# A one-layer RWKV and pooling trunk: the output projection's first weight chunks put into the stream's list, its input loaded within its loop through six buffers, and the embedding's fetch moved back

## The chip, the cores and the metric

The kernel runs on one core of one Trainium2 chip. The metric is the device time of one execution in microseconds; lower is better. The time before is 1112.82 us, the median of three runs (1111.49 to 1113.38).

## The reference, cut to what matters

One layer of a decoder trunk on a sequence of 512 positions with a model width of 2048, in float32:

```python
h = rms_norm(x, norm_g[i])
z = jnp.einsum('btd,dn->btn', h, w_in[i])
...
y = wkv7_scan(rh, wh, kh, vh, kk, ah)            # 16 heads x 64, delta-rule state
y = head_group_norm(y, ln_w[i], ln_b[i])
y_rwkv = (y + bonus.reshape(B, T, D_RWKV)).astype(dt) * jax.nn.silu(g_rwkv)
d = causal_multiscale_pool(u).astype(dt)
y_pool = jnp.einsum('btgc,gcd->btgd', d, w_pool[i]).reshape(B, T, D_POOL)
y_pool = y_pool * pool_scale[i] * jax.nn.silu(g_pool)
y_mix = jnp.concatenate([y_rwkv, y_pool], axis=-1)
x = x + jnp.einsum('btc,cd->btd', y_mix, w_out[i])
gate = jax.nn.sigmoid(jnp.einsum('btd,de->bte', x, w_pg[i]) + b_pg[i])
x = x + gate * jnp.einsum('btq,qd->btd', p[i], w_ple[i])
...
return rms_norm(x, final_g)
```

What matters here is the seam in the middle: `y_mix` (2048 channels by 512 positions) is multiplied by `w_out`, and the result feeds a second product with `w_pg`.

## The kernel before, in words

**Precision.** Each float32 operand of a large product is split in two float32r halves: ScalarE casts the high half (`nc.scalar.copy`, tiles named `whi`, `yhi`, `x2hi`), VectorE subtracts it to get the low half (`wlo`, `ylo`, `x2lo`). `mm3` (line 156 issues its matmuls) then does three matmuls: high by high, high by low, low by high. `wsplit` (lines 127 to 134) loads a weight chunk on SyncE's queue (L129) and splits it; it uses three tags of the pool `wp` (`raw`, `whi`, `wlo`) with four buffers each. `split` (lines 136 to 138) does the two halves for anything else.

**First stage.** x is normalised, transposed and split into `hhi` and `hlo`, 16 chunks of 128 channels by 512 positions. A *stream* then computes the columns of z in units of 128 channels: 16 chunks of 3 matmuls each per unit (`zk`, `zr`, `zv`, `zg` for the RWKV part, `zb` for the pooling part), and among them the embedding product (`pple`, `embed_unit`). The weight chunks of the whole stream stand in the list `plan`, and `chunk` takes them from its head: it loads and splits until the wanted chunk is ready, and two more. `plan` ends with the chunks of `b15` and `wp15`, the last pooling unit.

**Second stage, laid into the first.** For each of 8 pairs of heads (j = 0 to 7) the scan runs in chunks of 64 positions. Its small matmuls wait on VectorE, ScalarE and DMAs, so between them `pump(n)` issues n matmuls of the stream; the n are the constants H1 to H5, HE, HT, HX and the triple HC. `scores(j)` issues the products `pbo` and 32 matmuls `pm` that need the tile `bk` from VectorE (L599), and stores masks (`mt`) to DRAM for the triangular inverse (`invert`). It is called once ahead of the loop and then in `between`, after `pump(H3)` and before `pump_to(H2)`; `pump_to` rounds to a boundary that the sum of the pumps decides. Within this stage matmuls keep the order of the program (`pin`).

**The mixed output y.** Each finished piece goes to the DRAM tensor `yd`: a pooling unit through `sgp` (one buffer, L432), a pair of heads through `yo` (L860). 16 pieces of 128 channels by 512 positions, 256 KB each. The pooling units 14 and 15 end the stream, so their pieces are last in the list `order` = 8 to 13, 0 to 7, 14, 15.

**Third stage, the output projection** (`proj` with `w_out`, tiles `acc_o`): four column blocks `ec` of 512 columns. For each, 16 weight chunks in the sequence of `order`; for each chunk 4 row tiles by 3 matmuls, 12 in all. Weight chunks are loaded by `wsplit` in `proj`. The input comes back from `yd` with `load_y`: a DMA into `yin` (three buffers), then the split into `yhi` and `ylo`, which hold all 16 pieces. The first four loads are issued on SyncE's queue ahead of the stream's last pump (`pump(10 ** 6)`), the other twelve on ScalarE's queue behind it. After each block x is added, the sum is stored (`x2d`) and turned (`turn`: transposes `px` and a split into `x2hi`, `x2lo`).

**Fourth stage, the gate** (`proj` with `w_pg`, tiles `acc_g`): again four blocks. The turn of the last output block is laid behind the third chunk of the first gate block (`aside`). `recall` fetches a block of the embedding product back from DRAM (`pler`, four DMAs on ScalarE's queue, L971); block 0 is fetched after the last output block's sums in the program.

**Order.** A scheduler sets the order on each engine from the program's order, its dependences and its buffers; an instruction can so stand well ahead of its place in the text. In the built program the fetch of block 0 stands on ScalarE's queue ahead of the first cast of y. `tc.issue_after` puts what is issued in its block behind a named instruction of the same engine.

Of the kernel before, what the change touches and what calls it, by code (L numbers as in the profile page):

```python
# [9 lines left out]
F32 = mybir.dt.float32  # L10
# [5 lines left out]
P = 128  # L16
T = 512
D = 2048
KT = D // P
# [15 lines left out]
def trunk_kernel(ctx: ExitStack, tc: tile.TileContext, x, p, norm_g, w_in, mu, w0, w_up, a0, a_up,  # L35
                 k_k, k_a, r_k, ln_w, ln_b, w_pool, pool_scale, w_out, w_ple, w_pg, b_pg, final_g, out):
    nc = tc.nc
    PSUM = bass.MemoryType.PSUM
    x, p, w_in, w_out, w_ple, w_pg = x[0], p[0, 0], w_in[0], w_out[0], w_ple[0], w_pg[0]
    out = out[0]  # L40
# [93 lines left out]
        return hi, lo  # L134

    def split(hi, lo, src):
        nc.scalar.copy(hi, src)
        nc.vector.tensor_tensor(lo, src, hi.bitcast(F32), ALU.subtract)


    def rsqrt(y, v, t):
# [27 lines left out]
    plan, ready = [], {}  # L169
# [5 lines left out]
    def chunk(nm, c, ahead=2):  # L175
        while (nm, c) not in ready or ahead > 0:
            if (nm, c) in ready:
                ahead -= 1
            if not plan:
                break  # L180
            n_, c_, src, kt, w_ = plan.pop(0)
            if (n_, c_) not in ready:
                ready[n_, c_] = wsplit(src, kt, w_, f"{n_}_{c_}")
        return ready.pop((nm, c))

    yd = dram.tile([KT, P, T], F32, name="yd", bufs=1)
# [6 lines left out]
    EC = 512  # L193
# [12 lines left out]
    for kind, nm, j in jobs:  # L206
        if kind == "z":
            plan_cols({"r": O_R, "k": O_K, "v": O_V, "g": O_G}[nm] + j * P, f"{nm}{j}")
        elif kind == "p":
            continue  # L210
        elif kind == "e":
            for k in range(2):
                plan.append((f"e{j}_{k}", 0, w_ple[k * P:(k + 1) * P, j * EC:(j + 1) * EC].unsqueeze(1), 1, EC))
        else:
            g, i = j // 4, j % 2
            if j % 4 < 2:
                plan_cols(O_U + g * 256 + i * P, f"b{j}")
            else:
                plan_cols(O_GP + g * 256 + i * P, f"b{j}")
                plan.append((f"wp{j}", 0, w_pool[0, g, :, i * P:(i + 1) * P].rearrange("(k p) n -> p k n", p=P), 2, P))  # L220

    lraw = []

# [42 lines left out]
    pt = psM.tile([P, T], F32, name="pt_prm", tag="m")  # L266
# [38 lines left out]
    pt = psM.tile([P, T], F32, name="pt_prm", tag="m")  # L305
# [202 lines left out]

    pws, kks, late = {}, {}, [None]

    H1, H2, H3, H4, H5, HE = 6, 16, 16, 8, 13, 32

    def decay_and_rate(j):

# [390 lines left out]
    ymp = sy.enter_context(tc.tile_pool(name="ymp", bufs=1))  # L905
    yhi = ymp.tile([P, KT, T], F32R, name="yhi")
    ylo = ymp.tile([P, KT, T], F32R, name="ylo")
    order = [8, 9, 10, 11, 12, 13, 0, 1, 2, 3, 4, 5, 6, 7, 14, 15]

    def load_y(k, queue):  # L910
        t_ = ymp.tile([P, T], F32, name=f"yin{k}", tag="yin", bufs=3)
        queue.dma_start(out=t_, in_=yd[k])
        split(yhi[:, k, :], ylo[:, k, :], t_)

    for k in order[:4]:
        load_y(k, nc.sync)
    pump(10 ** 6)
    pin[0] = False
    for k in order[4:]:
        load_y(k, nc.scalar)  # L920


    x2hi = hp.tile([P, KT, T], F32R, name="x2hi", tag="ahi")
# [2 lines left out]
    KEEP = 8  # L926
# [8 lines left out]
    def proj(w, hi_, lo_, ec, nm, ks=range(KT), tts=range(NT), keep=None, aside=None):  # L935
        acc = {tt: acc_tile(f"acc_{nm}{ec}_{tt}") for tt in tts}
        if keep is not None:
            acc = {tt: [acc[tt]] if tt < NT - 1 else [acc[tt][:, 0:EC // 2], acc_tile("acc_h")[:, 0:EC // 2]]
                   for tt in tts}
        for i, k in enumerate(ks):  # L940
            src = w[k * P:(k + 1) * P, ec * EC:(ec + 1) * EC].unsqueeze(1)
            if keep is None or i < KT - KEEP:
                wh, wl = wsplit(src, 1, EC, f"{nm}{ec}_{k}")
            else:
                raw = wp.tile([P, 1, EC], F32, name=f"raw_{nm}{ec}_{k}", tag="raw")
                nc.sync.dma_start(out=raw, in_=src)
                own = i < KT - 4
                wh = (kp_ if own else wp).tile([P, 1, EC], F32R, name=f"whk{k}", tag=f"whk{k}" if own else "whi")
                wl = (kp_ if own else wp).tile([P, 1, EC], F32R, name=f"wlk{k}", tag=f"wlk{k}" if own else "wlo")
                split(wh, wl, raw)  # L950
                keep[k] = (wh, wl)
                continue
            for tt in tts:
                ts_ = slice(tt * P, (tt + 1) * P)
                parts = acc[tt] if keep is not None else [acc[tt]]
                hw = EC // len(parts)
                for h, a_ in enumerate(parts):
                    hc = slice(h * hw, h * hw + hw)
                    e_ = mm3(a_, hi_[:, k, ts_], lo_[:, k, ts_], wh[:, 0, hc], wl[:, 0, hc], i == 0, i == KT - 1)
            if aside is not None and i == 2:  # L960
                with tc.issue_after(e_.ins):
                    aside()
        return acc

    ples = {}

    def recall(ec, pool):
        ples[ec] = []
        for tt in range(NT):
            t_ = pool.tile([P, EC], F32, name=f"pler{ec}_{tt}", tag="ple", bufs=4)  # L970
            nc.scalar.dma_start(out=t_, in_=pled[tt * P:(tt + 1) * P, ec * EC:(ec + 1) * EC])  # L971
            ples[ec].append(t_)

    for ec in range(D // EC):
        es = slice(ec * EC, (ec + 1) * EC)
        acc = proj(w_out, yhi, ylo, ec, "o", order)
        x2 = []
        for tt in range(NT):
            rows = slice(tt * P, (tt + 1) * P)
            t_ = pp.tile([P, EC], F32, name=f"x2_{ec}_{tt}", tag=("u", "sw")[tt // 2])  # L980
            nc.scalar.dma_start(out=t_, in_=x[rows, es])
            nc.vector.tensor_tensor(t_, acc[tt], t_, ALU.add)
            nc.scalar.dma_start(out=x2d[rows, es], in_=t_)
            x2.append(t_)
        if ec == D // EC - 1:
            recall(0, lp)

        def turn(ec=ec, x2=x2):
            for i in range(EC // P):
                pt = psM.tile([P, T], F32, name=f"px2_{ec}_{i}", tag="m")  # L990
                for tt in range(NT):
                    nc.tensor.transpose(pt[:, tt * P:(tt + 1) * P], x2[tt][:, i * P:(i + 1) * P], ident)  # L992
                split(x2hi[:, 4 * ec + i, :], x2lo[:, 4 * ec + i, :], pt)


        if ec < D // EC - 1:
            turn()
# [4 lines left out]
    with tc.tile_pool(name="fp", bufs=2) as fp, tc.tile_pool(name="kp_", bufs=1) as kp_:  # L1002
# [83 lines left out]
            pre[tt] = (x2_, ple[tt])  # L1086

        for ec in range(LAST):
            ple = ples.pop(ec)
            pre = {}  # L1090
            vec = vectors(ec)
            acc = proj(w_pg, x2hi, x2lo, ec, "g", aside=turn if ec == 0 else None)
            recall(ec + 1, fp if ec % 2 == 0 else lp)
            for tt in range(NT):
                fetch(ec, tt)
                gate(acc[tt], ec, tt, slice(ec * EC, (ec + 1) * EC), ec)
# [60 lines left out]
```

## Time and profile before

| what | value |
|---|---|
| median of three runs | 1112.82 us |
| the profiled execution | 1113.69 us |
| its span, first to last instruction | 1112.0 us |
| TensorE busy | 1076.4 us (97%) |
| VectorE busy | 709.1 us (64%) |
| ScalarE busy | 449.7 us (40%) |
| granted TensorE clock, mean | 0.994 |
| mean DMA rate | 125 GB/s |

One execution is profiled; its own time is the one that terms worked out from its rows belong to. An engine's busy time says little by itself: what counts is where TensorE, the fullest engine, stood still and what it waited for. The views used are the list of waits, the chain of work that ended last (followed back from the last instruction), the timelines of single engines in a window (start, duration, engine, line, operation; in brackets how long the engine was idle before and what ended that), and the table of stretches, whose columns are the length, the busy time and number of instructions of TensorE, its weight loads, VectorE, ScalarE and GpSimd, then the granted clock, the DMAs' share and their rate. A letter q behind an engine's name marks its queue: a wait or the issue of a DMA.

### The profile page before, as it was taken

To read this page: it belongs to the slowest core of one execution; us is meant where nothing else is said; L and a number is where in the kernel's file an instruction comes from. 1 tells how busy PE (TensorE), PEld (TensorE's weight loads), DVE (VectorE), ACT (ScalarE), POOL (GpSimd) and SP (SyncE) were. 2 spreads that over 40 slices of the span, in tenths; PEclk is the share of its full clock that TensorE was granted. 3 is DMA by queue.
4 is the path that set the end of the run, shared out by engine and by line. 5 is a ranking of instruction groups with operands and counts; after the bars stand their busy time and mean duration, and the time that the engine had idled before them with its cause. 6 is when DMAs were issued, how large, how long until landed. Compare 5 with 4: busy or idle time off the path is not lost.

```text
span 1112.0 us, 17260 instructions
## 1 busy us (share of the span) xinstructions
PE 1076.4 (97%) x6090; PEld 879.9 (79%) x6090; DVE 709.1 (64%) x1835; ACT 449.7 (40%) x917; POOL 77.8 (7%) x180
## 2 busy tenths in 40 slices
PE   5999999999999999999999999979999999999996
PEld 4888887887877877877878788768888888888885
DVE  6677868778589688787885957453433324345266
ACT  7633435335335344353352344543222222333246
POOL 2100110110110001201101101000000000000000
PEclk9999999999999999999999999989999999999998
DMA  7433333333423332324234343774434437355444
GB/s 230 119 90 97 102 105 79 103 95 81 119 81 101 103 88 83 98 68 114 76 101 114 88 127 105 241 245 138 162 99 167 155 111 228 111 192 150 135 134 152
DMA packets 178486, 138.56 MB, mean 125 GB/s; under 512 B 34678, under 2 KB 139743, under 8 KB 178399
## 3 DMA queue, kind: packets, MB, share of 16 engines
q1 hardware_dynamic: 158270, 104.94, 32.1%
q10 hardware_dynamic: 20128, 32.52, 9.3%
q8 instruction: 48, 0.79, 0.3%
q14 instruction: 40, 0.32, 0.1%
HBM read 118.02 MB, written 18.87 MB: 123 GB/s over the span
## 4 chain that ended last, share of the span: by engine, by line
PE 48%; ACT 2%; DMA 2%; DVE 1%; issue 0%; ACTq 0%; SPq 0%
PE acc_o L156 16%; PE acc_g L156 14%; PE zb L156 8%; PE pple L156 2%; DMA yin<-yd 1%; PE zr L156 1%; PE zg L156 1%; PE zv L156 1%; PE zk L156 1%; PE py L156 1%; PE px L992 1%; PE pu L156 1%; PE pp L156 1%; ACT L1039 0%; PE ps L156 0%; PE pm L156 0%
## 5 line engine op out<-in xcount | busy, mean ns | idle before, releaser
L133 DVE TENSOR_TENSOR wlo_g<-raw_g,whi_g 128x512 fp32r<-128x512 f32 x88 | 59.6, 685 | 86.2 <-ACT whi_g L132 84.4
L133 DVE TENSOR_TENSOR wlo_o<-raw_o,whi_o 128x512 fp32r<-128x512 f32 x64 | 43.9, 691 | 101.4 <-ACT whi_o L132 101.4
L156 PE MATMUL zb<-hhi,whi_b 128*128 128x512 f32 x256 | 107.0, 418 | 0.0
L156 PE MATMUL acc_o<-whi_o,yhi 128*128 128x512 f32 x256 | 100.2, 395 | 6.8 <-ACT whi_o L132 6.8
L132 ACT CAST whi_g<-raw_g 128x512 fp32r<-128x512 f32 x88 | 54.4, 621 | 115.7 <-PE acc_g L156 71.5
L156 PE MATMUL acc_o<-whi_o,ylo 128*128 128x512 f32 x256 | 100.9, 394 | 0.0
L156 PE MATMUL acc_o<-wlo_o,yhi 128*128 128x512 f32 x256 | 100.5, 393 | 0.0
L156 PE MATMUL zb<-hhi,wlo_b 128*128 128x512 f32 x256 | 100.5, 393 | 0.0
L156 PE MATMUL zb<-hlo,whi_b 128*128 128x512 f32 x256 | 99.9, 390 | 0.0
L156 PE MATMUL acc_g<-whi_g,x2hi 128*128 128x512 f32 (+1 forms) x224 | 86.7, 387 | 0.0
L156 PE MATMUL acc_g<-wlo_g,x2hi 128*128 128x512 f32 (+1 forms) x224 | 86.4, 386 | 0.0
L156 PE MATMUL acc_g<-whi_g,x2lo 128*128 128x512 f32 x224 | 86.0, 386 | 0.0
L132 ACT CAST whi_o<-raw_o 128x512 fp32r<-128x512 f32 x64 | 39.9, 624 | 107.4 <-PE acc_o L156 105.2
L810 POOL TENSOR_SCALAR s0p<-sbd,pw 64x64 f32<-64x64 f32 x96 | 55.9, 582 | 324.0 <-DVE sbd L803 257.7
L132 ACT CAST whi_b<-raw_b 128x512 fp32r<-128x512 f32 x64 | 39.7, 621 | 85.0 <-PE zv L156 34.0
L133 DVE TENSOR_TENSOR wlo_b<-raw_b,whi_b 128x512 fp32r<-128x512 f32 x64 | 43.7, 685 | 33.5 <-ACT whi_b L132 33.2
L156 PEld LDWEIGHTS acc_o<-whi_o,yhi 128*128 128x128 f32 x256 | 48.5, 190 | 16.9 <-ACT whi_o L132 7.2
L156 PEld LDWEIGHTS zb<-hhi,wlo_b 128*128 128x128 f32 x256 | 48.0, 188 | 11.0
L156 PEld LDWEIGHTS acc_o<-wlo_o,yhi 128*128 128x128 f32 x256 | 48.6, 190 | 10.2
L156 PEld LDWEIGHTS acc_o<-whi_o,ylo 128*128 128x128 f32 x256 | 48.6, 190 | 10.0
L655 DVE TENSOR_TENSOR xw<-xw,tm 128x60 f32<-128x60 f32 (+24 forms) x248 | 52.0, 210 | 7.0
L156 PEld LDWEIGHTS zb<-hhi,whi_b 128*128 128x128 f32 x256 | 48.3, 189 | 8.7
(283 smaller groups left out, 2542.7 us busy)
## 6 DMA issues: line engine op xcount, KB each, us to landing
raw_b<-in_w_in_dram SPq DMA_DIRECT2D x64, 256.0 KB
raw_o<-in_w_out_dram SPq DMA_DIRECT2D x64, 256.0 KB
raw_g<-in_w_pg_dram SPq DMA_DIRECT2D x64, 256.0 KB
raw_k<-in_w_in_dram SPq DMA_DIRECT2D x32, 256.0 KB
raw_r<-in_w_in_dram SPq DMA_DIRECT2D x32, 256.0 KB
raw_v<-in_w_in_dram SPq DMA_DIRECT2D x32, 256.0 KB
raw_g<-in_w_in_dram SPq DMA_DIRECT2D x32, 256.0 KB
n<-nd SPq DMA_DIRECT2D x16, 256.0 KB
```

Source lines behind the costliest of these rows:

```text
L132: nc.scalar.copy(hi, raw)
L133: nc.vector.tensor_tensor(lo, raw, hi.bitcast(F32), ALU.subtract)
L156: i = nc.tensor.matmul(*a, **k)
L655: nc.vector.tensor_tensor(xw[:, 0:n_, s + 1:32], xw[:, 0:n_, s + 1:32], tm[:, 0:n_, 0:w_], ALU.add)
L810: nc.gpsimd.tensor_scalar(s0p[hc, :], nxt[hc, hc], pcn[hc], None, ALU.mult)
L992: nc.tensor.transpose(pt[:, tt * P:(tt + 1) * P], x2[tt][:, i * P:(i + 1) * P], ident)
```

## The change

The change has four parts.

1. The first four chunks of `w_out` (8, 9, 10, 11 of block 0) are appended to `plan`, so that `chunk` loads and splits them behind `wp15`; `proj` takes them from there.
2. `load_y` always issues on ScalarE's queue, `yin` has six buffers, and only the first six loads are issued ahead of the stream's last pump. The other ten are issued within the first block's loop, each six chunks ahead of its use.
3. H2 goes from 16 to 12 and H3 from 16 to 20.
4. The fetch of the embedding's block 0 moves from the last output block into the first gate block, behind the last cast of the turn (`split` and `turn` return it).

```diff
     def split(hi, lo, src):
-        nc.scalar.copy(hi, src)
+        c_ = nc.scalar.copy(hi, src)
         nc.vector.tensor_tensor(lo, src, hi.bitcast(F32), ALU.subtract)
+        return c_
...
+    order = [8, 9, 10, 11, 12, 13, 0, 1, 2, 3, 4, 5, 6, 7, 14, 15]
+    for k in order[:4]:
+        plan.append((f"o0_{k}", 0, w_out[k * P:(k + 1) * P, 0:EC].unsqueeze(1), 1, EC))
...
-    H1, H2, H3, H4, H5, HE = 6, 16, 16, 8, 13, 32
+    H1, H2, H3, H4, H5, HE = 6, 12, 20, 8, 13, 32
...
-    order = [8, 9, 10, 11, 12, 13, 0, 1, 2, 3, 4, 5, 6, 7, 14, 15]
-
-    def load_y(k, queue):
-        t_ = ymp.tile([P, T], F32, name=f"yin{k}", tag="yin", bufs=3)
-        queue.dma_start(out=t_, in_=yd[k])
+    AHEAD = 6
+
+    def load_y(k):
+        t_ = ymp.tile([P, T], F32, name=f"yin{k}", tag="yin", bufs=AHEAD)
+        nc.scalar.dma_start(out=t_, in_=yd[k])
         split(yhi[:, k, :], ylo[:, k, :], t_)
 
-    for k in order[:4]:
-        load_y(k, nc.sync)
+    for k in order[:AHEAD]:
+        load_y(k)
     pump(10 ** 6)
     pin[0] = False
-    for k in order[4:]:
-        load_y(k, nc.scalar)
...
-            if keep is None or i < KT - KEEP:
+            if nm == "o" and ec == 0 and i + AHEAD < KT:
+                load_y(ks[i + AHEAD])
+            if (f"{nm}{ec}_{k}", 0) in ready:
+                wh, wl = ready.pop((f"{nm}{ec}_{k}", 0))
+            elif nm == "o" and ec == 0 and i < 4:
+                wh, wl = chunk(f"{nm}{ec}_{k}", 0)
+            elif keep is None or i < KT - KEEP:
                 wh, wl = wsplit(src, 1, EC, f"{nm}{ec}_{k}")
...
             if aside is not None and i == 2:
                 with tc.issue_after(e_.ins):
-                    aside()
+                    hi = aside()
+                with tc.issue_after(hi.ins):
+                    recall(0, lp)
...
-        if ec == D // EC - 1:
-            recall(0, lp)
-
         def turn(ec=ec, x2=x2):
...
-                split(x2hi[:, 4 * ec + i, :], x2lo[:, 4 * ec + i, :], pt)
+                hi = split(x2hi[:, 4 * ec + i, :], x2lo[:, 4 * ec + i, :], pt)
+            return hi
```

What this does to the order on the engines is shown at three places. The names carry the piece or chunk: `yin12` is the load of piece 12 of y, `whi_o0_9` the high half of chunk 9 for block 0 of the output projection (in the new kernel a chunk of the list has one more number behind it).

ScalarE at the seam, before. The cast of the first chunk, `whi_o0_8`, stands seventeen rows ahead of the cast of the second; these are the last twelve, down to `whi_o0_9`:

```order
L912 DMA yin0_8106<-yd_136 128x512
L912 DMA yin1_8110<-yd_136 128x512
L367 ACTIVATE sgp15_8086<-zb15_8037 128x512
L912 DMA yin2_8114<-yd_136 128x512
L137 CAST yhi_7989<-yin0_8106 128x512
L137 CAST yhi_7989<-yin1_8110 128x512
L432 DMA yd_136<-sgp15_8086 128x512
L137 CAST yhi_7989<-yin2_8114 128x512
L912 DMA yin3_8118<-yd_136 128x512
L912 DMA yin4_8122<-yd_136 128x512
L912 DMA yin5_8126<-yd_136 128x512
L132 CAST whi_o0_9_8173<-raw_o0_9_8171 128x512
```

ScalarE at the same place, now, from the first chunk's cast to the fourth's:

```order
L132 CAST whi_o0_8_0_4871<-raw_o0_8_0_4869 128x512
L918 DMA yin12_8031<-yd_136 128x512
L137 CAST yhi_8013<-yin11_8027 128x512
L918 DMA yin13_8035<-yd_136 128x512
L132 CAST whi_o0_9_0_4921<-raw_o0_9_0_4919 128x512
L137 CAST yhi_8013<-yin12_8031 128x512
L438 DMA yd_136<-sgp14_8057 128x512
L137 CAST yhi_8013<-yin13_8035 128x512
L918 DMA yin0_8137<-yd_136 128x512
L132 CAST whi_o0_10_0_4927<-raw_o0_10_0_4925 128x512
L373 ACTIVATE sgp15_8118<-zb15_8069 128x512
L132 CAST whi_o0_11_0_4955<-raw_o0_11_0_4953 128x512
```

The casts of the four chunks now stand among the casts of the first six pieces of y, and the loads that follow are issued one by one between them. The store of `sgp14` has come behind the cast of piece 12; before it stood ahead of the casts of y.

ScalarE a little later, before, from the fourth chunk's cast to the sixth's:

```order
L132 CAST whi_o0_11_8209<-raw_o0_11_8207 128x512
L137 CAST yhi_7989<-yin6_8130 128x512
L137 CAST yhi_7989<-yin7_8134 128x512
L132 CAST whi_o0_12_8227<-raw_o0_12_8225 128x512
L137 CAST yhi_7989<-yin14_8138 128x512
L912 DMA yin15_8142<-yd_136 128x512
L132 CAST whi_o0_13_8245<-raw_o0_13_8243 128x512
```

ScalarE there now, from the cast of piece 0 to the sixth chunk's cast:

```order
L137 CAST yhi_8013<-yin0_8137 128x512
L918 DMA yin2_8169<-yd_136 128x512
L438 DMA yd_136<-sgp15_8118 128x512
L137 CAST yhi_8013<-yin1_8153 128x512
L918 DMA yin3_8185<-yd_136 128x512
L137 CAST yhi_8013<-yin2_8169 128x512
L918 DMA yin4_8201<-yd_136 128x512
L132 CAST whi_o0_12_8207<-raw_o0_12_8205 128x512
L137 CAST yhi_8013<-yin3_8185 128x512
L918 DMA yin5_8223<-yd_136 128x512
L137 CAST yhi_8013<-yin4_8201 128x512
L132 CAST whi_o0_13_8229<-raw_o0_13_8227 128x512
```

All loads of y but one stood ahead of the fifth chunk's cast (`whi_o0_12`) before; now the loads of pieces 3 and 4 stand just ahead of it, and the loads from piece 5 on behind it.

TensorE behind the seventh call of `scores` (j = 6), before; `pm6` are the last of its matmuls, `zk7` is the stream, whose weight chunk `whi_k7_0` ends here and `whi_k7_1` begins:

```order
L156 MATMUL pm6_10_6130<-ar6_6065,bk6_6066 128x128
L156 MATMUL pm6_11_6131<-ar6_6065,bk6_6066 128x128
L156 MATMUL zk7_6112<-hhi_134,whi_k7_0_3386 128x512
L156 MATMUL zk7_6112<-hlo_135,whi_k7_0_3386 128x512
L156 MATMUL zk7_6112<-hhi_134,wlo_k7_0_3387 128x512
L156 MATMUL zk7_6112<-hhi_134,whi_k7_1_3428 128x512
```

TensorE behind the same call, now:

```order
L157 MATMUL pm6_10_6157<-ar6_6089,bk6_6090 128x128
L157 MATMUL pm6_11_6158<-ar6_6089,bk6_6090 128x128
L157 MATMUL zk7_6136<-hhi_134,whi_k7_1_3428 128x512
L157 MATMUL zk7_6136<-hlo_135,whi_k7_1_3428 128x512
L157 MATMUL zk7_6136<-hhi_134,wlo_k7_1_3429 128x512
```

The last step of `whi_k7_0`, three matmuls, has moved from behind `scores` to ahead of it. One step of the stream moves so at all eight calls; the scan's next product behind it, `py`, stands where it stood.

More of the change, by code (lines that the diff above doesn't have):

```diff
@@ L1088, in trunk_kernel @@
         for ec in range(LAST):
-            ple = ples.pop(ec)
             pre = {}
@@ L1092, in trunk_kernel @@
             acc = proj(w_pg, x2hi, x2lo, ec, "g", aside=turn if ec == 0 else None)
+            ple = ples.pop(ec)
             recall(ec + 1, fp if ec % 2 == 0 else lp)
```

## The prediction

> **What bounds the kernel now.** I read the page first, then the chain that ended last, the waits of TensorE, and the timelines of TensorE, ScalarE and SyncE around the one long wait.
>
> ```profile
> span 1112.0 us, 17260 instructions
> PE 1076.4 (97%) x6090; PEld 879.9 (79%) x6090; DVE 709.1 (64%) x1835; ACT 449.7 (40%) x917; POOL 77.8 (7%) x180
> ```
>
> TensorE (PE) is busy 97% of the span, so all that an edit of order can give lies in the other 3%, 35.6 us, and in stretches where the clock is not full. The profiled execution took 1113.69 us, 1.7 more than its span and 0.9 more than the median of the runs, 1112.82. I make the sum against the profiled time and carry the difference over to the median.
>
> TensorE's waits, longest first (total, times, longest):
>
> ```profile
> PE pt_prm L267 <- DMA ngr<-in_norm_g_dram: 7.0, 1, 7.0
> PE acc_o L156 <- ACT whi_o L132: 6.8, 1, 6.8
> PE pt_h L279 <- DVE xt L263: 3.1, 2, 1.6
> PE pm L156 <- DVE bk L599: 2.3, 3, 1.5
> PE pu L156 <- DVE zs L781: 1.1, 4, 0.4
> ```
>
> The first and the third are the kernel's start, which the change leaves alone. The second is the start of the output projection, where it works; the fourth is `scores`, which H2 and H3 move; the fifth is the scan just behind it. So the change can take away 9.1 us of waiting, and what hangs on it.
>
> The chain over the seam of the two stages (start, duration, what):
>
> ```profile
> 720.89 3.66 DMA yd<-yo
> 725.07 0.42 SPq L912
> 725.54 6.92 DMA yin<-yd
> ...
> 738.91 3.59 DMA yin<-yd
> ...
> 744.27 0.63 ACT whi_o L132
> 744.94 43.26 PE acc_o L156 x180
> ...
> 792.58 41.07 PE acc_o L156 x181
> ```
>
> The chain runs from loads of y through their casts on ScalarE into the cast of a weight chunk. The timeline of TensorE shows which:
>
> ```profile
> 735.28 0.39 PE L156 MATMUL acc_o<-whi_o,yhi 128*128 128x512 f32 x1
> ...
> 744.94 2.08 PE L156 MATMUL acc_o<-whi_o,yhi 128*128 128x512 f32 x4 [6.78 <-ACT whi_o L132]
> ...
> 749.96 0.39 PE L156 MATMUL acc_o<-whi_o,yhi 128*128 128x512 f32 x1
> ```
>
> The projection starts at 735.28 without a wait, does its first chunk, stands still for 6.78, does the second, and begins the third at 749.96. The stretches 738 to 745, 745 to 750 and 750 to 755 (last columns: clock, DMA share, GB/s) say what follows the wait:
>
> ```profile
> 738.00:745.00 7.00, 0.22 (x2) 0.06 (x1) 4.23 (x7) 3.23 (x6) 0.00 (x0) 0.84 0.61 215
> 745.00:750.00 5.00, 5.00 (x13) 3.95 (x14) 3.50 (x6) 2.99 (x5) 0.00 (x0) 0.54 0.75 211
> 750.00:755.00 5.00, 5.00 (x24) 4.14 (x23) 4.23 (x7) 3.39 (x6) 0.00 (x0) 1.00 0.77 265
> ```
>
> After the wait the granted clock is 0.54 for 5 us. A full-speed pitch is 41.07 / 181 = 0.227 us, so two chunks of 12 matmuls cost 5.45. They took 749.96 - 735.28 = 14.68. **The seam costs 9.23 us**: 6.8 of waiting and 2.4 of slow clock.
>
> **The output projection's chunks.** The wait is one of order. In the old order seventeen rows of ScalarE stand between the casts of the first chunk and the second: eight loads of y (which wait for one of three buffers), six casts of y (which wait for landings), a fetch, a store and `sgp15`. In the new order it is three, and the third and fourth chunk follow after four rows and one. The six first loads go out on ScalarE's queue from 724.71, where the embedding's fetch went, under the same wait (for the store of `yo`, which lands at 720.89 + 3.66 = 724.55). SyncE's row, then ScalarE's:
>
> ```profile
> 724.69 1.28 SPq L912 DMA_DIRECT2D yin<-yd  x3
> ...
> 724.71 0.83 ACTq L971 DMA_DIRECT2D pler<-pled  x2
> ...
> 726.13 0.37 ACTq L971 DMA_DIRECT2D pler<-pled  x1
> 730.07 0.62 ACT L137 CAST yhi<-yin 128x512 fp32r<-128x512 f32 x1 [3.54 <-DMA yin<-yd]
> 731.15 0.62 ACT L137 CAST yhi<-yin 128x512 fp32r<-128x512 f32 x1 [0.46 <-DMA yin<-yd]
> 732.48 0.62 ACT L137 CAST yhi<-yin 128x512 fp32r<-128x512 f32 x1 [0.72 <-DMA yin<-yd]
> 733.01 0.62 ACT L132 CAST whi_o<-raw_o 128x512 fp32r<-128x512 f32 x1
> ```
>
> Three loads as late as now would put the first chunk's cast at 733.01 as now, and TensorE starts at 735.28 again. The second chunk's cast needs one more load, sent when the first has landed (row order: cast of yin8, load of yin11). What one trip from issue to cast takes, three at a time:
>
> ```profile
> 732.63 0.33 ACTq L912 DMA_DIRECT2D yin<-yd  x1
> 733.86 0.33 ACTq L912 DMA_DIRECT2D yin<-yd  x1
> 736.53 0.62 ACT L137 CAST yhi<-yin 128x512 fp32r<-128x512 f32 x1 [0.56 <-DMA yin<-yd]
> 737.54 0.62 ACT L137 CAST yhi<-yin 128x512 fp32r<-128x512 f32 x1 [0.38 <-DMA yin<-yd]
> 742.58 1.66 ACTq L912 DMA_DIRECT2D yin<-yd  x3
> 745.33 1.28 ACT L137 CAST yhi<-yin 128x512 fp32r<-128x512 f32 x2 [0.44 <-DMA yin<-yd]
> ```
>
> 3.9, 3.7 and, with less in flight, 2.75; the chain has 3.59. The first load of the burst at 724.7 took 5.4, the third 6.92. So chunk 9 is cast at 724.71 + 5.4 + 3.7 + 0.1 + 0.55 (a cast's pitch) = 734.5 and split by VectorE 1.3 later, 735.8; TensorE wants it at 735.28 + 2.72 = 738.0. Chunk 10, one trip further, is cast by about 739.3 and chunk 11 by 741.6; they are wanted at 740.7 and 743.45. The store of `sgp14` now goes out behind the cast of yin12, at about 736.8, and `sgp15`, in the same buffer, waits the 3.66 that a store takes, with chunk 11 behind it; that is in the 741.6.
>
> **The new wait.** Each later load is issued from the same in-order queue, behind a cast that waits for an earlier load. Chunk 12 hangs on five trips one after another (yin8, 11, 13, 0, 2): 724.71 + 5.4 + 4 x 3.7 + 4 x 0.1 = 745.3, then two casts, 746.5, and VectorE's half, 747.2 (727.0 + 5 L, if every trip takes L). TensorE would want that half at 735.28 + 4 x 2.72 + 0.23 = 746.4: **0.8 lost**. Chunk 13 needs one more trip (yin4, issued with the cast at 745.3), 3.7 for a chunk of 2.72: **1.0 lost** (L - 2.72). From there two loads are in flight at a time, one per 1.9 us, faster than a chunk's 2.72, so it ends. Three of the embedding's four fetches, each as large as a load of y, leave the burst, so its first trip should come nearer to 4.4, which takes the loss to 0.8. Bounds: none at all at 2.75 a trip; about 4.5 if the first takes 6.92 and the others 3.9. I take 1.5, between 0.8 and 1.8, nearer to the rows as they stand. A wait of this size does not slow the clock: after TensorE's wait of 1.51 before `pm` the next matmuls run at 3.62 / 15 = 0.24 us.
>
> ```profile
> 512.04 2.06 PE pm L156 x32
> 514.09 3.62 PE zk L156 x15
> ```
>
> The Trainium skill ("DMA: Bandwidth & Descriptors", section "Issuing engines are not separate DMA queues") says that all issuers share the same 16 DMA engines, and that another issuer only saves the sequencer's issue time. That speaks against this part: the loads' move to ScalarE buys no bandwidth and puts four more issues on the engine that casts. By it the trips stay as the rows have them and the sum stands; if a queue of their own made them 2.75, the 1.5 would go and the sum would be 1102.1. No row here compares the two queues alone.
>
> SyncE loses its four y loads and sends chunks 10 and 11 earlier, which costs nothing. GpSimd has no part in it.
>
> **H2 and H3.** Of 32 matmuls around `scores`, one step of three moves ahead of it, 0.68 us, at eight places. Where `pm` waits for `bk`, the step fills the wait:
>
> ```profile
> 436.34 1.83 PE L156 MATMUL pm<-ar,bk 64*128 64x128 f32 x28 [0.62 <-DVE bk L599]
> 512.04 2.06 PE L156 MATMUL pm<-ar,bk 64*128 64x128 f32 x32 [1.51 <-DVE bk L599]
> ```
>
> The third of the three is 0.2. Gain 0.62 + 0.68 + 0.2 = **1.5 us**. Behind `scores` the masks on VectorE end 0.7 later while `py` stays where it was; the scan's `zs` comes behind them, and TensorE waits for it 1.1 in all today. I take nothing for that. Bounds: from a loss of 1.1, those waits doubled and nothing gained, to the 1.5.
>
> **The embedding's fetch.** Four issues of about 0.4 move on ScalarE to behind the last turn, ahead of the cast of the gate's chunk 7:
>
> ```profile
> 935.24 0.59 ACT L137 CAST x2hi<-px 128x512 fp32r<-128x512 f32 x1
> 937.36 0.62 ACT L132 CAST whi_g<-raw_g 128x512 fp32r<-128x512 f32 x1 [1.53 <-PE acc_g L156]
> 969.20 1.23 ACT L1034 ACTIVATE gt<-gt 128x512 f32<-128x512 f32 x2 [1.36 <-DVE gt L1033]
> ```
>
> That cast waits for the slot of chunk 3; chunks 4 to 6 give TensorE 8 us in which 1.7 are hidden. The fetched tiles are used at 969, over 25 us after. Nothing.
>
> **Sum.** 9.23 (seam) + 1.5 (`scores`) - 1.5 (new waits) = 9.2 us less: 1113.69 becomes 1104.5, and the median 1112.82 becomes **1103.6**.
>
> **Rivals.** (1) *Trips of about 4.5 us.* Then chunk 12 waits 727.0 + 5 x 4.5 - 746.4 = 3.1, chunk 13 another 1.8, and the first wait may be long enough to slow the clock again (2.4). Loss 7.3: 1112.82 - 9.23 - 1.5 + 7.3 = 1109.4. For it: the burst had 5.4 to 6.9, so a trip grows with what is in flight. Against: the y loads quoted after the burst took 3.9 at most. The trace leaves open where between 1.51 and 6.78 the clock gives way. The Trainium skill ("TensorE: Matmul & The Clock Gate", section "What's actually happening") puts it at an idle window of about 3.4 us; by that rule the clock would stay and this case would end at 1107.0.
>
> (2) *The load chain becomes the bound; slower.* Its place is ScalarE's queue from yin11 to yin15. With each trip at L, chunks 12 and 13 lose 6 L - 22.1, and the clock 2.4; that equals the 10.7 gained at L = 5.07. At 6.1, which the burst's second load took (from 725.07 to the cast at 731.15), the loss is 16.9: 1119.0. From 5.4 on, two loads in flight no longer keep up with 2.72 a chunk. Against it: the same rows as in (1), and three fetches fewer in the burst.
>
> (3) *No change.* Trips of just about 5 us give the gain back, or the first chunk itself comes late because it now stands behind casts of y whose loads ScalarE issues. That would need the first cast some 9 us later than 733.01, with fewer transfers ahead of it than now. 1112.8.
>
> **Chances.** Forecast 0.76, with its own range 1101.5 to 1108.1; (1) 0.13; (2) 0.05; (3) 0.06. The bottom is the gain without a new wait, 1102.1, less some of the spread of the runs (1111.49 to 1113.38). The top is 4.5 of waiting and nothing from H3: 1112.82 - 4.7 = 1108.1. That leaves out half of (1), (2) and (3), under 2 in 10. About 0.2%, 2.2 us, is what a measurement of this kernel can tell from no change; faster by more 0.89, within it 0.06, slower 0.05.
>
> **What would show it.** In the new profile: TensorE's wait for `whi_o` of 6.8 gone and no stretch at 0.54 near 745; in its place waits under 1.5 for `whi_o` or `wlo_o` at the fifth and sixth chunk; `pm` waiting 0.8 in all for `bk`; trips of 3 to 4 us from an issue of `yin` to its cast. It is wrong if a single wait of over 3 us stands in the first projection, if the trips take over 4.5, or if TensorE waits anew behind `scores`.

## The result and the profile after

| kernel | median | range | profiled span | mean clock |
|---|---|---|---|---|
| before, beside these runs | 1113.1 us | 1111.49 to 1115.0 | 1112.0 us | 0.994 |
| changed | 1103.03 us | 1102.61 to 1103.82 | 1101.5 us | 0.997 |

The ratio is 0.9904, with a 95% interval from 0.9892 to 0.9917: the change takes 9.2 to 12.0 us away. The changed kernel's profiled execution took 1103.22 us.

Its page, and TensorE's waits in it (total, times, longest):

```profile
span 1101.5 us, 17252 instructions
PE 1074.0 (98%) x6090; PEld 878.4 (80%) x6090; DVE 708.1 (64%) x1835; ACT 448.8 (41%) x917; POOL 77.7 (7%) x180
```

```profile
PE pt_prm L273 <- DMA ngr<-in_norm_g_dram: 6.7, 1, 6.7
PE pt_h L285 <- DVE xt L269: 3.2, 2, 1.6
PE pu L157 <- DVE zs L787: 1.1, 4, 0.4
...
PE pm L157 <- DVE bk L605: 0.8, 1, 0.8
```

The wait of `acc_o` for `whi_o` is gone from the list, and no other wait of `acc_o` is in it. `pm` waits once, 0.8, where it waited three times, 2.3. The scan's 1.1 is as it was, and the two waits of the kernel's start nearly so (6.7 and 3.2; before 7.0 and 3.1). The chain now crosses the seam on TensorE alone, and the stretches around it have the full clock (columns as before; clock, DMA share and GB/s last):

```profile
732.40 1.36 PE pp L157 x6
733.76 43.52 PE acc_o L157 x192
```

```profile
737.00:744.00 7.00, 7.00 (x32) 5.82 (x31) 4.48 (x7) 3.43 (x7) 0.00 (x0) 1.00 0.89 272
744.00:749.00 5.00, 5.00 (x23) 4.13 (x22) 3.78 (x7) 3.56 (x7) 0.00 (x0) 1.00 0.68 209
749.00:754.00 5.00, 5.00 (x24) 4.13 (x23) 2.75 (x6) 2.19 (x4) 0.00 (x0) 1.00 0.74 237
```

43.52 / 192 = 0.227 us, the full-speed pitch from the first chunk on. Where TensorE was busy 0.22 of 7.00 us before, it is busy 7.00 of 7.00.

The matmuls of one kind show the length of the whole projection, by the starts of the first and the last; before, then changed:

```profile
L156 PE MATMUL acc_o<-whi_o,ylo x256: 388/389/628, 735.7 to 924.1; 128*128 128x512 f32 x128
```

```profile
L157 PE MATMUL acc_o<-whi_o,ylo x256: 389/389/481, 734.0 to 913.2; 128*128 128x512 f32 x128
```

By TensorE's timelines, from the start of the first matmul of `acc_o` to that of the last, it is 188.87 us before and 179.63 changed. So the span's 10.46 us split like this: 9.24 inside the projection, 1.68 ahead of it (first matmul at 735.28, now 733.60; the stream's first matmuls start within 0.02 us of each other), and 0.46 lost behind it (from the last matmul to the end 187.82, now 188.28).

### The profile page after: what moved, and what is told of

It reads as the page before. It is cut to its first block, busy times and chain, and to the rows that moved or that the text cites. A ratio compares the mean times of both kernels' runs of the same rounds, so it can differ in the third digit from the quotient of the medians.

```text
span 1101.5 us, 17252 instructions
## 1 busy us (share of the span) xinstructions
PE 1074.0 (98%) x6090; PEld 878.4 (80%) x6090; DVE 708.1 (64%) x1835; ACT 448.8 (41%) x917; POOL 77.7 (7%) x180
## 4 chain that ended last, share of the span: by engine, by line
PE 67%; DVE 4%; ACT 3%; DMA 1%; issue 1%; ACTq 0%; DVEq 0%
PE acc_o L157 16%; PE acc_g L157 13%; PE zb L157 13%; PE zg L157 5%; PE zk L157 4%; PE zr L157 4%; PE zv L157 2%; PE py L157 2%; PE pu L157 1%; PE pp L157 1%; PE pm L157 1%; PE pple L157 1%; DMA pled<-ple 1%; PE ps L157 1%; DVE xw L661 1%
```

## The experiments

Each is read by its median and by the length of the projection as just defined, which is that of its one profiled execution. The ratio is to runs of the kernel before that were taken beside the experiment; their median was 1113.82 us for e1 to e4, 1114.05 for e5 to e8 and 1113.71 for e9 to e12, and 1113.1 beside the changed kernel. So a difference between medians of two such groups can be off by up to about 0.9 us.

| run | what it is | median, us | ratio to before, 95% interval | projection, us |
|---|---|---|---|---|
| changed | all four parts | 1103.03 | 0.9892 to 0.9917 | 179.63 |
| e1 | list alone | 1109.5 | 0.9945 to 0.997 | 184.51 |
| e2 | loop and six buffers alone | 1106.18 | 0.9916 to 0.9941 | 180.30 |
| e3 | changed, H2 and H3 as before | 1104.34 | 0.9898 to 0.9925 | 179.63 |
| e4 | H2 and H3 alone | 1112.8 | 0.9976 to 0.9994 | 189.83 |
| e5 | list, fetch | 1106.99 | 0.9921 to 0.9948 | 182.38 |
| e6 | list, six buffers | 1114.82 | 0.9999 to 1.0017 | 189.24 |
| e7 | changed, more DMA traffic | 1115.39 | 0.9997 to 1.0015 | 188.52 |
| e8 | changed, H2, H3 = 8, 24 | 1104.37 | 0.9903 to 0.993 | 180.15 |
| e9 | changed, fetch in its old place | 1103.55 | 0.9892 to 0.9919 | 180.15 |
| e10 | changed, three buffers | 1102.63 | 0.9889 to 0.9916 | 179.63 |
| e11 | list, six buffers, fetch | 1111.08 | 0.9958 to 0.9982 | 186.32 |
| e12 | changed, H2, H3 = 10, 22 | 1102.7 | 0.9887 to 0.9914 | 179.75 |

The theory is the prediction's: what counts is the order of ScalarE, that is, how many casts of y, each hanging on a landing, stand ahead of the cast of the weight chunk that TensorE wants next. The rivals are the transfers themselves (their length in the burst) and the number of buffers.

### e1: the list alone

```diff
+    for k in order[:4]:
+        plan.append((f"o0_{k}", 0, w_out[k * P:(k + 1) * P, 0:EC].unsqueeze(1), 1, EC))
...
+            if (f"{nm}{ec}_{k}", 0) in ready:
+                wh, wl = ready.pop((f"{nm}{ec}_{k}", 0))
+            elif nm == "o" and ec == 0 and i < 4:
+                wh, wl = chunk(f"{nm}{ec}_{k}", 0)
```

> The kernel before with the first part of the change alone: the four weight chunks end the stream's list; y is loaded as before (three buffers, four loads on SyncE), H2 and H3 and the fetch are as before. Theory (order): the 6.8 us wait was the second chunk's cast standing behind y loads and y casts that were not needed yet; in this kernel's order the casts of chunks 8 to 11 stand right behind the casts of pieces 10, 10, 13 and 13, so the wait goes, with at most 2 us left around chunks 12 and 13; about 9 us faster than before, 1104 (the 1.5 us of H2 and H3 are not in it). Rival (transfers): the relief came from the loads of y being sent one by one through six buffers and from the fetch having left the burst, so that trips became short; then with three buffers and the fetch in the burst the trips stay at 3.6 to 6.9 us and a wait of 4 us or more remains in the seam; at most 5 us faster, 1108 or more.

It brought 4.36 of the 9.24 us (188.87 to 184.51); 4.88 stayed. TensorE's timeline has two waits for a chunk's cast, at the sixth and at the eighth chunk; the chain shows what the first hangs on:

```profile
750.65 0.51 PE L156 MATMUL acc_o<-whi_o,yhi 128*128 128x512 f32 x1 [1.66 <-ACT whi_o L132]
...
757.94 0.50 PE L156 MATMUL acc_o<-whi_o,yhi 128*128 128x512 f32 x1 [0.82 <-ACT whi_o L132]
```

```profile
725.81 8.00 DMA yin<-yd
733.84 0.63 ACT yhi L137
...
742.92 5.29 DMA yin<-yd
748.24 0.63 ACT yhi L137
```

The list holds four chunks; behind it the casts of y decide again, and the third load of the burst took 8.00 us from issue to landing. So "order alone" was too simple: with long trips the wait comes back four chunks later, though in a smaller size. The time, 1109.5, is the one that the rival named (1108 or more), but without its wait of 4 us or more. The idle times, with those for `wlo_o`, sum to 3.2, but 4.88 were lost. A matmul takes 0.39 and the next starts 0.227 behind it, so a wait, which is counted from the end of the last matmul, costs 0.16 more than it shows; five waits make 0.8. The rest is lost in the matmuls just behind each wait, of which the first takes 0.5 and a later one starts about 0.1 late.

### e2: the loop and six buffers alone

```diff
-        t_ = ymp.tile([P, T], F32, name=f"yin{k}", tag="yin", bufs=3)
-        queue.dma_start(out=t_, in_=yd[k])
+        t_ = ymp.tile([P, T], F32, name=f"yin{k}", tag="yin", bufs=AHEAD)
+        nc.scalar.dma_start(out=t_, in_=yd[k])
...
+            if nm == "o" and ec == 0 and i + AHEAD < KT:
+                load_y(ks[i + AHEAD])
```

> The kernel before with the second part alone: y loaded in the loop through six buffers on ScalarE, no chunks in the list, H2, H3 and fetch as before. Theory (order): in this kernel's order the first chunk's cast stands behind the cast of piece 13, three trips down the chain (4.8 + 2.7 + 2.9 us from 724.7, then the cast and VectorE's half), so TensorE waits 1 to 2.5 us ahead of the first chunk and up to 1 us at the next two; 6 to 8 us faster than before, 1105 to 1107. Rival (transfers): all of the relief comes from this part; no wait over 0.5 us, 9 us faster, 1104.

The first chunk's cast stands behind six casts of y, and TensorE waits for it (the view says only "issue", but that cast runs from 735.54 to 736.16):

```profile
736.26 0.47 PE L156 MATMUL acc_o<-whi_o,yhi 128*128 128x512 f32 x1 [0.99 <-issue]
737.02 0.50 PE L156 MATMUL acc_o<-wlo_o,yhi 128*128 128x512 f32 x1 [0.29 <-DVE wlo_o L133]
```

Behind that there is no wait, as the order theory had it, and 1106.18 lies in its range. So the loop alone takes most of the seam, and the list is worth what is left: 1106.18 - 1104.34 (e3, which adds list and fetch) = 1.8 us.

### e3 and e4: H2 and H3

```diff
-    H1, H2, H3, H4, H5, HE = 6, 12, 20, 8, 13, 32
+    H1, H2, H3, H4, H5, HE = 6, 16, 16, 8, 13, 32
```

> The changed kernel with H2 and H3 back at 16 and 16. Theory: TensorE's wait of pm for bk is 2.3 us again in three places instead of 0.8 in one, everything else as in the changed kernel: 1.5 us slower than the changed kernel, about 1104.5. Rival: what H2 and H3 take from pm they give back elsewhere (masks later on VectorE, so zs or the casts later): 0.5 us or less between the two.

```diff
-    H1, H2, H3, H4, H5, HE = 6, 16, 16, 8, 13, 32
+    H1, H2, H3, H4, H5, HE = 6, 12, 20, 8, 13, 32
```

> The kernel before with H2 = 12 and H3 = 20 alone. Theory: 1.5 us faster than before, pm's wait 0.8 us in one place, the seam's wait of 6.8 us untouched. Rival: 0.5 us or less.

Given the rest, the two numbers are worth 1104.34 - 1103.03 = 1.3 us by the medians, whose ranges lie apart. They are of two such groups, and by the ratios it is 0.9 with overlapping intervals; in the traces both projections are 179.63 long, and the changed kernel's starts 1.51 earlier (735.11 to 733.60), though its stream starts 0.2 later. Alone the two numbers are worth 0.7 to 2.7 us by the ratio. In e4's trace the projection starts 1.9 earlier than before (733.38; 0.3 of it is there at the start of the stream), and its long wait then is 7.05 instead of 6.78 long: a part of what is gained ahead of an unmended wait is lost in it.

### e5: list and fetch

e1, with the fetch behind the turn, as in the change's fourth part.

> The kernel before with the list's four chunks and the embedding's fetch moved back, but three buffers, the loads of y in front of the loop and H2, H3 = 16, 16. The list alone took 1109.5 us: 4.9 us of the seam's 9.2 were still there, in waits of TensorE at the second, sixth and ninth chunk, and the first three trips of y took 6.0, 7.5 and 8.0 us beside four fetches of the embedding. Theory 'burst': the fetches in the burst make those trips long and put the three-buffer chain late; without them the first trips are 4.5 to 5.5 us, the waits go, and the time is 1104 to 1106 us (the changed kernel with H2, H3 = 16, 16 took 1104.34). Rival 'three buffers': each load must wait for a cast to free its buffer, so the chain stays late whatever lies beside it; waits of 2 us or more stay and the time is 1108 to 1110 us.

1106.99 lies between the two theories, and each holds in part. The burst's first trips fell to 4.3, 4.9 and 5.1 us, and 2.1 of e1's 4.88 went. The rest is one wait at the eighth chunk:

```profile
750.13 0.33 ACTq L915 DMA_DIRECT2D yin<-yd  x1
...
755.32 0.62 ACT L137 CAST yhi<-yin 128x512 fp32r<-128x512 f32 x1 [2.77 <-DMA yin<-yd]
...
755.99 0.62 ACT L137 CAST yhi<-yin 128x512 fp32r<-128x512 f32 x1
756.51 1.14 ACT L132 CAST whi_o<-raw_o 128x512 fp32r<-128x512 f32 x2
```

Here fifteen of the sixteen casts of y stand ahead of the eighth chunk's cast, for which TensorE waits 1.0. (The expectation above has e1's waits at the second, sixth and ninth chunk; they are at the third, sixth and eighth.)

### e6 and e11: six buffers without the loop

```diff
-        t_ = ymp.tile([P, T], F32, name=f"yin{k}", tag="yin", bufs=3)
+        t_ = ymp.tile([P, T], F32, name=f"yin{k}", tag="yin", bufs=6)
```

> The kernel before with the list's four chunks and six buffers for y, with the loads still in front of the loop, the fetch at its old place and H2, H3 = 16, 16. ScalarE's order then has the cast of the fifth chunk (12) behind the casts of fifteen of the sixteen tiles of y. Theory 'burst and order': the first trips stay at 6 to 8 us, and the fifth chunk waits for fifteen trips; from the third landing about 9.5 us after the first issue and then one tile in about 1.25 us, the fifth chunk's halves are ready some 25 us after the first issue, about 4 us after TensorE wants them: 1108 to 1112 us, with the wait at the fifth chunk. Rival 'three buffers': the buffers were what held the list back, and the time is 1104 to 1106 us with no wait over 0.5 us.

> The kernel before with the list, six buffers and the fetch moved back, H2, H3 = 16, 16 and the loads of y in front of the loop: all of the change but the loop. ScalarE's order has the cast of the fifth chunk (12) behind fourteen tiles of y. Theory 'order': with list and six buffers alone the fourteenth tile landed 27.4 us after the first was issued, and TensorE waited 7.1 us at the fifth chunk; first trips that are 2 us shorter bring that to some 4 to 5 us: 1108 to 1112 us, slower than with three buffers (1107.0). Rival 'fetch and buffers': both together free the loads, and the time is 1104 to 1106 us.

More buffers made it slower, by 5.3 us against e1 and by 4.1 against e5. ScalarE in e6, ahead of the wait at the fifth chunk, then TensorE there:

```profile
750.50 0.62 ACT L137 CAST yhi<-yin 128x512 fp32r<-128x512 f32 x1 [1.32 <-DMA yin<-yd]
...
752.04 1.27 ACT L137 CAST yhi<-yin 128x512 fp32r<-128x512 f32 x2 [0.92 <-DMA yin<-yd]
753.22 1.13 ACT L132 CAST whi_o<-raw_o 128x512 fp32r<-128x512 f32 x2
```

```profile
753.88 2.07 PE L156 MATMUL acc_o<-whi_o,yhi 128*128 128x512 f32 x4 [7.08 <-ACT whi_o L132]
```

In e11 it is the same place with a shorter wait:

```profile
750.21 2.08 PE L157 MATMUL acc_o<-whi_o,yhi 128*128 128x512 f32 x4 [4.10 <-ACT whi_o L132]
```

With the loads in front of the loop, buffers that are free let the scheduler put fifteen casts of y (e6) or fourteen (e11) ahead of the fifth chunk's cast, where three buffers had let it put eight (e1) or nine (e5). This is the wait of before, moved on by three chunks. So the row at which the cast stands decides where TensorE waits. How long it waits hangs on the trips as well: e1, with eight casts ahead, is slower than e5 with nine. e11 came out as its theory had it. e6's theory had the place, but a wait of about 4 us; it was 7.08, with a granted clock of 0.52 from 754 to 758 behind it, and the time missed the 1108 to 1112.

### e7: more traffic

```diff
+        d_ = ymp.tile([P, 1024], F32, name=f"fl{k}", tag="fl", bufs=2)
+        nc.gpsimd.dma_start(out=d_, in_=w_pg[k * P:(k + 1) * P, 0:1024])
         nc.scalar.dma_start(out=t_, in_=yd[k])
```

> The changed kernel with one more load of 512 KB on GpSimd's queue for each of the sixteen loads of y, into a tile that nothing reads; ScalarE's order is as in the changed kernel. It prices the second rival: what longer trips do. Measured trips of the five that the fifth chunk hangs on were 4.7, 2.6, 2.9, 3.9 and 2.9 us, with nothing waiting. Theory: the margin at the fifth chunk was about 3 us, so trips longer by 1 us each (L from 3.1 to over 4) already eat it, and beyond that each 1 us of trip costs about 5 us at the fifth chunk; trips of 4.5 to 6 us are expected, and 1106 to 1120 us, with waits of TensorE at the fifth and later chunks. Rival: the sixteen engines serve the y loads ahead, trips stay under 4 us, and the time is within 1.5 us of 1103.

The order is the changed kernel's, only the DMA engines are full (share 1.01, 368 GB/s, against 0.85 and 268 in the same stretch of the changed kernel):

```profile
734.00:744.00 10.00, 9.68 (x41) 7.23 (x40) 4.89 (x9) 3.41 (x6) 2.11 (x4) 1.00 1.01 368
...
754.00:758.00 4.00, 3.56 (x8) 2.55 (x9) 2.47 (x4) 1.62 (x4) 1.00 (x2) 0.57 0.98 340
```

```profile
747.66 0.50 PE L157 MATMUL acc_o<-whi_o,yhi 128*128 128x512 f32 x1 [1.65 <-ACT whi_o L132]
748.47 0.50 PE L157 MATMUL acc_o<-wlo_o,yhi 128*128 128x512 f32 x1 [0.31 <-DVE wlo_o L133]
754.43 0.80 PE L157 MATMUL acc_o<-whi_o,yhi 128*128 128x512 f32 x1 [3.17 <-ACT whi_o L132]
```

The five trips that the fifth chunk hangs on took 4.44, 5.32, 4.84, 4.52 and 4.14 us from issue to landing, 4.65 in the mean, and TensorE waits at the fifth and sixth chunk (and 0.3 at the fourth). The projection is 8.9 us longer than in the changed kernel, which eats the seam's gain: the second rival's mechanism, at its place. The weight chunks' loads are slower here too, but the casts that are waited for follow directly behind casts of y.

### e8 and e12: on from H2, H3 = 12, 20

> The changed kernel with H2, H3 = 8, 24 in place of 12, 20. From 16, 16 to 12, 20 the waits of pm for bk fell from 2.3 to 0.8 us and the time fell by 1.3 us. Theory: four more vectors' matmuls ahead of that wait take away the last 0.8 us (at 511 us) too, 0.7 to 1.1 us faster than the changed kernel: 1102.0 to 1102.4. Rival: 8 matmuls are too few behind which the casts and zs can hide, so a wait of pu or pp takes its place: 1103.0 us or more.

> The changed kernel with H2, H3 = 10, 22, between 12, 20 (1103.03 us, pm waits 0.8 us for bk) and 8, 24 (1104.37 us, no wait of pm, but py waits 0.73, 0.48, 0.48 and 0.48 us for mt). Two matmul columns are about 0.45 us of TensorE: pm's wait should fall to about 0.4 us and py's waits to about 0.3 us in all. Theory: the two nearly cancel, 1102.6 to 1103.4 us, not to be told from the changed kernel. Rival: both waits vanish, 1102.2 us or less, a better kernel.

e8's largest new wait, then what is left of `pm`'s in e12:

```profile
PE py L157 <- DVE mt L630: 2.2, 4, 0.7
```

```profile
PE pm L157 <- DVE bk L605: 0.2, 1, 0.2
```

At 8, 24 `pm` no longer waits, but `py` waits for the masks, which come later: 1.3 us slower than 12, 20 by the medians, with ranges that lie apart (1104.16 to 1105.77), though the ratios' intervals overlap. So the theory failed, and the rival's time came, with `py` in the place of `pu` or `pp`. At 10, 22 `py` does not wait for them and `pm` waits 0.2. Its median is 0.3 below the changed kernel's, with overlapping ranges (1102.56 to 1103.04 against 1102.61 to 1103.82), so it can't be called better.

### e9 and e10: the fetch in its old place; three buffers

```diff
-                    hi = aside()
-                with tc.issue_after(hi.ins):
-                    recall(0, lp)
+                    aside()
...
+        if ec == D // EC - 1:
+            recall(0, lp)
```

> The changed kernel with the embedding's fetch back at its old place in the code. Without the loop the fetch sat in the burst of the first loads, and moving it took 2.1 us of the list's waits away (1109.5 to 1107.0 us). With the loop, ScalarE's order has the four fetches behind the last load of y, between the casts of the last chunks. Theory (the prediction's 'embedding's fetch move: nothing'): with the loop in, the place of the fetch in the code changes nothing that TensorE waits for: 1102.5 to 1103.6 us, first trips of y as in the changed kernel (4.7, 5.0, 5.2 us). Rival: the fetch move carries a part of the gain here too, first trips of 6 us or more and 1104.5 to 1106 us.

```diff
-    AHEAD = 6
+    AHEAD = 3
```

> The changed kernel with three buffers for y in place of six, loads still in the loop, three chunks ahead. Theory 'order': what counts is that the cast of each chunk stands behind no more tiles of y than TensorE needs soon; the fifth chunk's cast is behind eight tiles here (ten in the changed kernel), with 8 us of matmuls between a load and its use, so three buffers are enough: 1102.6 to 1104.0 us, no wait of the output projection over 0.5 us. Rival 'buffers': the three buffers that left waits of 1.0 us and more in the kernel with list and fetch alone leave them here too: 1105 to 1107 us.

Neither can be told from the changed kernel (the fifth chunk's cast is behind nine tiles there, not ten as e10's expectation counts). In e9 the fetch stays out of the burst without being moved; ScalarE's timeline:

```profile
723.38 1.30 ACTq L918 DMA_DIRECT2D yin<-yd  x3
...
727.87 0.62 ACT L137 CAST yhi<-yin 128x512 fp32r<-128x512 f32 x1 [2.74 <-DMA yin<-yd]
...
754.17 0.33 ACTq L981 DMA_DIRECT2D pler<-pled  x1
```

Once y's loads stand in the loop on ScalarE's queue, the scheduler puts the fetch behind the last of them, 30 us later. So the fetch is worth 2.5 us (e1 to e5) or 3.7 (e6 to e11) where the loads stand in front of the loop, and nothing measurable where they stand in it. The same holds for the buffers: six cost 4 to 5 us without the loop, and with it three do as well.

## Why the prediction was right, point by point

The predicted 1103.6 is 0.6 above the measured median. The mechanism was right; one term was mis-sized. That the totals lie so near is in part luck. The sum rests on the profiled executions, and there 1104.5 stands beside 1103.22, some 1.3 off: the mis-sized term makes 1.5, but 0.46 was lost behind the projection, for which the sum has nothing. And the profiled execution of before lies 0.9 above its median, that of the changed kernel only 0.2.

**The seam, 9.23.** Measured 9.24 (188.87 to 179.63). That wait and slow clock had to be counted together is shown by the full clock in all three stretches above.

**H2 and H3, 1.5.** 1.3 between the medians of e3 and the changed kernel (0.9 by the ratios), and 1.68 by the projection's start against before. The two waits of 0.62 and 0.2 are gone and 1.51 became 0.82. Nothing was taken for what lies behind `scores`, and the scan's waits are 1.1 as before. e8 shows that this holds for one step: the next one turns into waits of `py`.

**The new waits, -1.5: the step that was mis-sized.** They are 0 in the changed kernel's trace. The step took 5.4 for the first trip and 3.7 for the others. ScalarE in the changed kernel, the five trips to chunk 12 (yin8, 11, 13, 0, 2):

```profile
723.02 1.31 ACTq L918 DMA_DIRECT2D yin<-yd  x3
...
727.77 0.62 ACT L137 CAST yhi<-yin 128x512 fp32r<-128x512 f32 x1 [3.00 <-DMA yin<-yd]
727.78 0.33 ACTq L918 DMA_DIRECT2D yin<-yd  x1
...
730.41 0.63 ACT L137 CAST yhi<-yin 128x512 fp32r<-128x512 f32 x1 [0.17 <-DMA yin<-yd]
730.42 0.33 ACTq L918 DMA_DIRECT2D yin<-yd  x1
...
733.37 0.62 ACT L137 CAST yhi<-yin 128x512 fp32r<-128x512 f32 x1 [0.92 <-DMA yin<-yd]
733.38 0.33 ACTq L918 DMA_DIRECT2D yin<-yd  x1
...
737.33 0.33 ACTq L918 DMA_DIRECT2D yin<-yd  x1
737.61 0.62 ACT L137 CAST yhi<-yin 128x512 fp32r<-128x512 f32 x1
...
740.22 0.63 ACT L137 CAST yhi<-yin 128x512 fp32r<-128x512 f32 x1
740.28 0.34 ACTq L918 DMA_DIRECT2D yin<-yd  x1
740.74 0.62 ACT L132 CAST whi_o<-raw_o 128x512 fp32r<-128x512 f32 x1
```

From issue to cast the first is 4.75, the next two 2.6 and 2.95; from 723.02 to 740.22 it is 17.2 where the step had 20.6. TensorE reaches the fifth chunk at 733.60 + 4 x 2.72 = 744.5, and its high half is there at 741.4: 3.1 us early (the low half, with which the step reckoned, at 742.2: 2.5 early). Three of the embedding's fetches were rightly taken out of the burst, but for the later trips the step used before's 3.7 to 3.9, which were measured with a late fetch and other loads of y beside them. In this trace the rows at the lower bound, 2.75, were nearer. It also let each issue go with its cast: yin2 was issued at 737.33, ahead of the cast of yin0 at 737.61, since that cast was still behind `whi_o`.

The margin of 2.5 us does not come with the order, though; it is in part luck. e3, e8, e9 and e12 have the same rows of casts and loads here, and in their traces the stretch that took 17.2 us takes 19.7, 20.0, 19.9 and 19.9, near the step's 20.6: the fifth trip (yin2) took 5.0 to 5.5 from issue to landing instead of 2.87. ScalarE in e9, then TensorE at the fifth chunk:

```profile
738.29 0.33 ACTq L918 DMA_DIRECT2D yin<-yd  x1
...
743.31 0.62 ACT L137 CAST yhi<-yin 128x512 fp32r<-128x512 f32 x1 [2.90 <-DMA yin<-yd]
...
743.84 0.62 ACT L132 CAST whi_o<-raw_o 128x512 fp32r<-128x512 f32 x1
```

```profile
745.31 0.50 PE L157 MATMUL acc_o<-wlo_o,yhi 128*128 128x512 f32 x1 [0.17 <-DVE wlo_o L133]
```

In e3 and e12 the low half is ready 0.35 and 0.1 us before TensorE wants it, in e8 and e9 0.3 after, which makes their projections 0.5 longer (180.15). So the term is 0 to 0.5 instead of 1.5. The 0.8 at the fifth chunk was off by 0.5 to 1.2 there; the 1.0 at the sixth came in none of these traces, since the sixth trip (yin4) took 2.5 to 2.6 in those four and not 3.7. Why the fifth trip differs so between traces of the same order stays open.

**The embedding's fetch, nothing.** Right in the sum (e9), but the reason was incomplete: the prediction put the shorter first trip down to the fetch's move, and in the changed kernel the loop alone brings it. A price of it may be in the tail. A new wait stands near its new place, at the transposes of the last turn:

```profile
PE px L1001 <- DVE x2lo L138: 0.3, 1, 0.3
```

The 0.46 lost behind the projection goes with this wait: the kernels that have it (0.33 us in the changed one, 0.26 in e11, 0.19 in e8, and 0.08 in e10) take 188.28, 188.25, 188.18 and 188.05 there, and all others 187.77 to 187.89. All four have the moved fetch, but so have e3, e5, e7 and e12, without the wait. So the place of this loss is shown; what makes `x2lo` late stays open.

**ScalarE's queue or SyncE's.** No row of before compared them. Now one does: e11 sends the burst on SyncE's queue with the fetch gone, and its three first trips took 4.3, 4.9 and 5.1 us; the changed kernel on ScalarE's queue has 4.7, 5.0 and 5.2. The Trainium skill ("DMA: Bandwidth & Descriptors", section "Issuing engines are not separate DMA queues") says that DMAs of all issuers run on the same 16 engines, and that a further issuer saves only the time to start them; as far as these trips go, the traces agree.

**Rival 1, the clock.** The prediction left open where between 1.51 and 6.78 it gives way. e1's wait of 1.66 left it at 1.00 behind it; behind e7's 3.17 it fell to 0.57 for 4 us, eight matmuls taking 754.43 to 758.14 = 3.7 instead of 1.8. So in these runs it lies between these. The Trainium skill ("TensorE: Matmul & The Clock Gate", section "What's actually happening") has an idle window of about 3.4 us; a wait that the trace gives as 3.17 was enough here. That wait is counted from an end that the profile models; from the start of the last matmul before it to the start of the next it is 754.43 - 750.87 = 3.56.

**Rival 2, the load chain.** Its price held: with the measured 4.65 a trip, 6 L - 22.1 is 5.8, and 2.4 of clock make 8.2; e7 lost 8.9. The parts fit less well than the sum: e7 begins the sixth chunk at 754.43 instead of 733.88 + 5 x 2.72 = 747.48, so 6.95 were lost where the formula has 5.8, since that chunk's own trip took 6.68, and the slow clock cost 1.9 instead of 2.4. At the changed kernel's mean of 3.40 (4.73, 2.61, 2.93, 3.87, 2.87 from issue to landing) the formula gives less than nothing, as measured. Break-even at 5.07 itself wasn't met: the profiled execution of e7 was its fastest, 1112.02 us, and the median of its runs, 1115.39, at before's level, has trips that no trace shows.

**The signs.** The wait of 6.8 and the slow stretch are gone, and `pm` waits 0.8, as the prediction named. The waits under 1.5 at the fifth and sixth chunk did not come. The trips from issue to cast were 2.6 to 5.2 and not 3 to 4; five of the sixteen took over 4.5, which the prediction would have counted against itself, and TensorE waited for none of them.

## What to carry to other kernels

Where an in-order engine both waits for landings and casts what the fullest engine wants next, count the rows ahead of each such cast in the built order: a list or more buffers alone only moved the wait here, and it went when loads and casts were laid out at the rate at which they are used. A trace without a wait says little about the margin; traces of other kernels with the same order showed it. More buffers in front of the loop cost 4 to 5 us here, because they gave the scheduler room to put the wrong casts first. Price a wait with its tail (1.7 us on top of 3.2 of idle in e1; in e7, at 3.17 us, the clock as well), and a transfer by what will be in flight beside it after the change, not before.

## What the runs showed of the hardware

One and the same load of 256 KB took 2.6 us from issue to landing outside a burst (yin11 in the changed kernel, with one or two other loads of y still under way), 4.1 to 5.5 in a burst of three, 5.35 to 8.0 with the embedding's fetches in that burst (before, e1, e4, e6), and up to 7.35 with an added stream of 8.4 MB (e7). A wait of TensorE costs more than its idle time even where the clock stays: 3.2 us of idle in e1 were 4.88 of delay, at a granted clock of 1.00.
